# Attention rows split into a near part and a residue-class part, with their weights exchanged through DRAM

## The chip, the core and the metric

The kernel runs on one core of a Trainium2 chip. The metric is device time in microseconds (us) of one launch. The engines are named as in the profile: PE (matmul), PEld (its weight loads), DVE (vector), ACT (activation), POOL, and SP, whose queue issues nearly all DMAs.

## What is computed

One transformer-like block for 1024 tokens of width 1024: an input projection, a gated depthwise convolution branch, an attention branch with 16 heads of 64, a gated merge, an output projection, and a convolutional feed-forward part. The change touches the attention alone. The reference runs three dilated windows for each head and mixes them by their log sums:

```python
DILATION_GROUPS = ((128, 1), (512, 4), (2048, 16))
...
for window, dilation in DILATION_GROUPS:
    o_g, lse_g = dilated_window_attention(q, k, v, slopes, window, dilation)
    outs.append(o_g)
    lses.append(lse_g)
mix = jax.nn.softmax(jnp.stack(lses), axis=0)
o = jnp.einsum('gbsh,gbshd->bshd', mix, jnp.stack(outs))
```

Mixing windows by their log sums is the same as one softmax over all earlier keys, in which a key counts once for each window that holds it. So a query at token i sees key j = i - d when d <= 128, or d is a multiple of 4 and d <= 512, or d is a multiple of 16. Both kernels put the count and the distance bias into one table, the mask, which holds -1e30 where no window holds the key.

## The kernel before

All matmul operands are kept as a high and a low part (`split`: ACT copies with rounding, DVE subtracts), so that a product takes two or three matmuls. Weights come through `stage` (DMA into one of four `raw` buffers) and `wsplit`. Programs are written in loops and a scheduler then orders each engine's instructions by its own timing model, so the order on an engine is that of the built program, not of the source.

The attention stage works head by head. `head(h)` loads q, kh, kl (six DMAs), the mask m (128x1024) and v. `score(h, tiles, i)` makes the scores of query block i (128 tokens) against all its (i+1)*128 earlier keys: matmuls of up to 512 columns, with q as stationary operand and kh, then kl, as moving one. One DVE instruction adds the mask and takes the extreme of the row, ACT takes exp and the row's sum, DVE the reciprocal, and POOL scales the row. `flip` turns a tile of 128 keys: PE transposes it for up to four query blocks into one PSUM bank, and `split` writes ph and pl. `weigh` multiplies v by ph and pl into o. `step` writes the order: the four scores of a half head (512 queries) are interleaved with the flips and weighings of the half head before, with `PEND` flips between a flip and its weighing.

Between these parts stands side work, `side_work`: the gate projections that are left and the conv-output projections, one step being three matmuls of 512 columns. `fill(n)` adds n to a credit and issues one step for each whole unit. The shares of side work are `FILL = (5.5, 9.5)` for the two halves, 15 steps per head; what is left over runs after the last head:

```python
        step(None, prev)
        for _ in filler:
            pass
```

After that the next stage loads o back (`load_split(oT, do_, half, "o")`, half 0 and then half 1, four `raw` buffers each), loads and splits `w_ao`, and multiplies (`yb`).

Of the kernel before, what the change touches and what calls it, by code (L numbers as in the profile page):

```python
# [12 lines left out]
F32 = mybir.dt.float32  # L13
F32R = mybir.dt.float32r
AF = mybir.ActivationFunctionType
ALU = mybir.AluOpType
# [4 lines left out]
P = 128  # L21
# [10 lines left out]

LAG = 2
PEND = 2
FILL = (5.5, 9.5)
COVER = (24, 16, 52)


# [12 lines left out]
def block_kernel(ctx: ExitStack, tc: tile.TileContext, x, g1, g2, pack, mask,  # L51
# [22 lines left out]
    def split(hi, lo, src):  # L74

        act.activation(hi, src, AF.Copy)  # L76
        dve.tensor_tensor(out=lo, in0=src, in1=hi.bitcast(F32), op=ALU.subtract)  # L77
# [54 lines left out]
    def fetch(dst, src):  # L132
        sp.dma_start(dst.bitcast(F32), src.bitcast(F32))


    dq = [[dr.tile([P, 4, T], F32R, name=f"dq{i}_{a}") for a in range(2)] for i in range(2)]
    dk = [[dr.tile([P, 4, T], F32R, name=f"dk{i}_{a}") for a in range(2)] for i in range(2)]
# [207 lines left out]
    with tc.tile_pool(name="ph2", bufs=1) as p2:  # L345
        def side_work():
            for t in gates:
                if t == "half":
                    aT = hb_tiles(hb1, "aT")
                    load_split(aT, da, 0, "a")  # L350
                yield
            load_split(aT, da, 1, "a")
            for c0 in (0, 4):
                ws = [wpiece(w_co[c], f"co{c}") for c in range(c0, c0 + 4)]
                for half in range(2):
                    for c in range(c0, c0 + 4):
                        yp = bank_ps(f"ya_{c}_{half}")
                        yield from gemm_half(yp, ws[c - c0], aT, half)
                        ya = cst.tile([P, 512], F32, tag="f2", bufs=2, name=f"ya_{c}_{half}")
                        act.activation(ya, yp, AF.Copy)  # L360
                        sp.dma_start(dya[c][:, half * 512 : half * 512 + 512], ya)

        def head(h):
            hp, r, g8 = h // 2, (h % 2) * DH, h // 8
            q = p2.tile([P, T], F32R, tag="q", bufs=2, name=f"q_{h}")
            kh = p2.tile([P, T], F32R, tag="kh", bufs=2, name=f"kh_{h}")
            kl = p2.tile([P, T], F32R, tag="kl", bufs=2, name=f"kl_{h}")
            m = p2.tile([P, T], F32, tag="m", bufs=2, name=f"m_{h}")
# [5 lines left out]
            sp.dma_start(m, mask[h])  # L374
            fetch(v, dv[h // 8][:, h % 8, :, :])
            return q, kh, kl, v, m

        def score(h, tiles, i):
            q, kh, kl, v, m = tiles
            nk = (i + 1) * P  # L380
            s = big_ps(f"s_{h}_{i}")
            for c0 in range(0, nk, 512):
                n = min(512, nk - c0)
                pe.matmul(s[:, c0 : c0 + n], q[:, i * P : (i + 1) * P], kh[:, c0 : c0 + n], start=True, stop=False)  # L384
                pe.matmul(s[:, c0 : c0 + n], q[:, i * P : (i + 1) * P], kl[:, c0 : c0 + n], start=False, stop=True)
            pt = p2.tile([P, nk], F32, tag=f"p{i}", bufs=1, name=f"p_{h}_{i}")
            st = p2.tile([P, 32], F32, tag="st", bufs=4, name=f"st_{h}_{i}")
            u0 = 896 - i * P
            dve.tensor_tensor_reduce(out=pt, in0=s[:, :nk], in1=m[:, u0 : u0 + nk], scale=-1.0, scalar=3e38,  # L389
                                     op0=ALU.add, op1=ALU.min, accum_out=st[:, 0:1])  # L390
            act.activation(pt, pt, AF.Exp, bias=st[:, 0:1], scale=-1.0, accum_out=st[:, 1:2])  # L391
            dve.reciprocal(st[:, 2:3], st[:, 1:2])  # L392
            pool.tensor_scalar(pt, pt, st[:, 2:3], 1.0, op0=ALU.mult, op1=ALU.mult)  # L393
            return pt

        def flip(h, half, pts, kt):
            q0 = max(0, kt - half * 4)
            pp = bank_ps(f"pp_{h}_{half}_{kt}")
            for qb in range(q0, 4):
                pe.transpose(pp[:, qb * P : (qb + 1) * P], pts[qb][:, kt * P : (kt + 1) * P], ident)  # L400
            ph = p2.tile([P, 512], F32R, tag="ph", bufs=4, name=f"ph_{h}_{half}_{kt}")
            pl = p2.tile([P, 512], F32R, tag="pl", bufs=4, name=f"pl_{h}_{half}_{kt}")
            c = slice(q0 * P, 512)
            split(ph[:, c], pl[:, c], pp[:, c])
            return kt, ph, pl, c

        def weigh(o, v, nkt, kt, ph, pl, c):
            pe.matmul(o[:, c], v[:, kt, :], ph[:, c], start=(kt == 0), stop=False)  # L408
            pe.matmul(o[:, c], v[:, kt, :], pl[:, c], start=False, stop=(kt == nkt - 1))  # L409
# [11 lines left out]
        opairs = {}  # L421

        def step(cur, prev):

            pts = []
            rate = FILL[0] / 14 if prev is not None and prev[1] else FILL[1] / 10
            if prev is not None:
                h, half, ppts, v = prev
                nkt = half * 4 + 4
                o = bank_ps(f"o_{h}_{half}")  # L430
                pend = []
            for n in range(4):
                if cur is not None:
                    pts.append(score(cur[0], cur[2], cur[1] * 4 + n))
                fill(rate)
                if prev is not None:
                    for kt in range(n * nkt // 4, (n + 1) * nkt // 4):
                        pend.append(flip(h, half, ppts, kt))
                        fill(rate)
                        if len(pend) > PEND:  # L440
                            weigh(o, v, nkt, *pend.pop(0))
            if prev is not None:
                while pend:
                    fill(rate)
                    weigh(o, v, nkt, *pend.pop(0))
                r = (h % 2) * DH
                if h % 2 == 0 and half == 0:
                    opairs[h // 2] = p2.tile([P, T], F32, tag="op", bufs=2, name=f"op_{h}")
                opair = opairs[h // 2]
                tmp = p2.tile([P, 512], F32, tag="ot", bufs=2, name=f"ot_{h}_{half}")  # L450
                act.activation(tmp[r : r + DH, :], o[DH:P, :], AF.Copy)
                dve.tensor_tensor(out=opair[r : r + DH, half * 512 : half * 512 + 512], in0=o[0:DH, :],
                                  in1=tmp[r : r + DH, :], op=ALU.add)
                if h % 2 == 1:
                    sp.dma_start(do_[:, h // 2, half * 512 : half * 512 + 512],
                                 opair[:, half * 512 : half * 512 + 512])
            return pts

        prev = None
        nxt = head(0)  # L460
        for h in range(H):
            cur = nxt
            for half in range(2):
                if half == 1 and h + 1 < H:
                    nxt = head(h + 1)
                pts = step((h, half, cur), prev)
                prev = (h, half, pts, cur[3])
        step(None, prev)
        for _ in filler:
            pass  # L470

# [337 lines left out]

def _mask():  # L810

    dist = np.arange(P)[:, None] + 896 - np.arange(T)[None, :]
    cnt = ((dist <= 128).astype(np.int64) + ((dist % 4 == 0) & (dist <= 512)) + (dist % 16 == 0)) * (dist >= 0)
    base = np.where(cnt > 0, np.log(np.maximum(cnt, 1)), 0.0)
    slopes = 2.0 ** (-8.0 * np.arange(1, H + 1) / H)
    m = base[None] - slopes[:, None, None] * dist[None]
    return np.where(cnt[None] > 0, m, -1e30).astype(np.float32)


def _layout(a):  # L820
# [38 lines left out]
```

## Time and profile before

| what | value |
|---|---|
| median of 3 runs | 1814.08 us (1813.51 to 1816.09) |
| the profiled execution | 1811.43 us, span 1809.6 us |
| mean granted TensorE clock | 0.991 |
| PE busy | 1765.8 us, 98% of the span |
| DVE, ACT, POOL busy | 1318.8, 771.6 and 195.8 us |
| DMA | 257.57 MB, mean 142 GB/s |
| attention stage, first score to first `yb` matmul | 549.6 to 976.9 us |

A page row names line, engine, operation, tiles written and read, shapes and count, then the busy time of the group, the mean of one in ns, and the idle time of the engine just before them with what ended it. Matmuls are pipelined and their records overlap, so durations of PE are not to be summed.

### The profile page before, as it was taken

To read this page: it belongs to the slowest core of one execution; us is meant where nothing else is said; L and a number is where in the kernel's file an instruction comes from. 1 tells how busy PE (TensorE), PEld (TensorE's weight loads), DVE (VectorE), ACT (ScalarE), POOL (GpSimd) and SP (SyncE) were. 2 spreads that over 40 slices of the span, in tenths; PEclk is the share of its full clock that TensorE was granted. 3 is DMA by queue.
4 is the path that set the end of the run, shared out by engine and by line. 5 is a ranking of instruction groups with operands and counts; after the bars stand their busy time and mean duration, and the time that the engine had idled before them with its cause. 6 is when DMAs were issued, how large, how long until landed. Compare 5 with 4: busy or idle time off the path is not lost.

```text
span 1809.6 us, 22474 instructions
## 1 busy us (share of the span) xinstructions
PE 1765.8 (98%) x8244; PEld 1461.9 (81%) x8244; DVE 1318.8 (73%) x1798; ACT 771.6 (43%) x1202; POOL 195.8 (11%) x197
## 2 busy tenths in 40 slices
PE   7999999999999999999999999989999999999999
PEld 5888888888887888887888878768888888878887
DVE  5999999999735655666654543787777777789863
ACT  4111132232245656666655332545444554543441
POOL 1000133133002122222210000210000000000000
PEclk9999999999999999999999999999999999999999
DMA  5111145345549456666527543313222222389851
GB/s 203 59 47 47 41 134 163 116 134 157 157 173 246 145 158 175 180 165 179 164 70 279 169 160 133 104 48 107 80 82 81 71 95 91 116 303 335 298 180 47
DMA packets 142063, 257.57 MB, mean 142 GB/s; under 512 B 11265, under 2 KB 60545, under 8 KB 141953
## 3 DMA queue, kind: packets, MB, share of 16 engines
q1 hardware_dynamic: 141808, 255.61, 43.8%
q8 instruction: 65, 1.06, 0.3%
q10 hardware_dynamic: 144, 0.52, 0.1%
q14 instruction: 46, 0.37, 0.1%
HBM read 190.03 MB, written 66.06 MB: 142 GB/s over the span
## 4 chain that ended last, share of the span: by engine, by line
PE 53%; DMA 4%; DVE 4%; issue 1%; ACT 1%; SPq 1%; POOLq 0%; POOL 0%; DVEq 0%; ACTq 0%
PE xz L550 5%; PE xz L551 5%; PE xz L552 5%; PE dx L703 5%; PE dy L703 5%; DMA gg<-dya 2%; PE pp L400 2%; PE y L550 2%; PE y L552 2%; PE y L551 2%; PE ya L108 2%; PE ya L109 2%; PE ya L110 2%; PE o L408 2%; PE wo L126 1%; PE wo L127 1%
## 5 line engine op out<-in xcount | busy, mean ns | idle before, releaser
L253 DVE SCALAR_TENSOR_TENSOR cacc<-apad,pk,cacc 128x1024 f32<-128x1024 f32 x240 | 297.7, 1274 | 0.7
L125 PE MATMUL qkv<-hi_qkv,hT 128*128 128x512 f32 x384 | 151.8, 396 | 0.0
L127 PE MATMUL qkv<-hi_qkv,hT 128*128 128x512 f32 x384 | 150.0, 391 | 0.0
L126 PE MATMUL qkv<-lo_qkv,hT 128*128 128x512 f32 x384 | 149.4, 390 | 0.0
L389 DVE CUSTOM_DVE_ANT_0 p<-s,m 128x128 f32<-128x128 f32 (+7 forms) x128 | 95.1, 750 | 62.7 <-PE pp L400 39.0
L77 DVE TENSOR_TENSOR pl<-pp,ph 128x512 fp32r<-128x512 f32 x192 | 103.1, 549 | 49.1 <-ACT ph L76 48.6
L393 POOL TENSOR_SCALAR p<-p,st 128x128 f32<-128x128 f32 (+7 forms) x128 | 94.9, 748 | 335.5 <-DVE st L392 211.9
L76 ACT ACTIVATE ph<-pp 128x512 fp32r<-128x512 f32 x192 | 91.3, 487 | 92.2 <-PE pp L400 89.3
L649 DVE SCALAR_TENSOR_TENSOR u<-u,pk 128x1023 f32<-128x1023 f32 (+1 forms) x88 | 112.3, 1279 | 18.9 <-ACT u L647 18.5
L101 POOL TENSOR_TENSOR rs<-ss,mhalf 128x8 f32<-128x8 f32 (+1 forms) x40 | 80.3, 2010 | 353.1 <-DVE ss L100 353.0
L391 ACT ACTIVATE p<-p,st 128x128 f32<-128x128 f32 (+7 forms) x128 | 99.0, 776 | 14.6 <-DVE st L389 12.9
L108 PE MATMUL gate<-hT,hi_gt 128*128 128x512 f32 x256 | 101.8, 398 | 0.0
L109 PE MATMUL gate<-hT,hi_gt 128*128 128x512 f32 x256 | 100.8, 394 | 0.0
L110 PE MATMUL gate<-hT,lo_gt 128*128 128x512 f32 x256 | 100.3, 393 | 0.0
L400 PE MATMUL pp<-ident,p 128*128 128x128 f32 x576 | 94.4, 277 | 0.0
L127 PEld LDWEIGHTS qkv<-hi_qkv,hT 128*128 128x128 f32 x384 | 72.0, 188 | 15.3
L126 PEld LDWEIGHTS qkv<-lo_qkv,hT 128*128 128x128 f32 x384 | 72.2, 188 | 14.5 <-DVE lo_qkv L77 0.3
L125 PEld LDWEIGHTS qkv<-hi_qkv,hT 128*128 128x128 f32 x384 | 72.2, 188 | 14.0
L400 PEld LDWEIGHTS pp<-ident,p 128*128 128x128 f32 x576 | 69.5, 142 | 10.0 <-issue 0.2
L384 PE MATMUL s<-kh,q 128*128 128x512 f32 (+1 forms) x192 | 69.7, 368 | 7.3 <-DVE st L389 4.8
L408 PE MATMUL o<-ph,v 128*128 128x512 f32 x192 | 73.1, 381 | 3.6 <-ACT ph L76 1.8
L409 PE MATMUL o<-pl,v 128*128 128x512 f32 x192 | 70.5, 369 | 1.6 <-DVE pl L77 1.5
(269 smaller groups left out, 4610.4 us busy)
## 6 DMA issues: line engine op xcount, KB each, us to landing
wr<-w_down SPq DMA_DIRECT2D x45, 512.0 KB, 5.7
gr<-dff SPq DMA_DIRECT2D x62, 256.0 KB, 5.2
raw_qkv<-w_qkv SPq DMA_DIRECT2D x24, 512.0 KB, 3.9
raw_uv<-w_up SPq DMA_DIRECT2D x22, 512.0 KB, 3.3
raw_ug<-w_up SPq DMA_DIRECT2D x22, 512.0 KB, 3.3
dff<-u SPq DMA_DIRECT2D x22, 512.0 KB, 2.6
dv<-v SPq DMA_DIRECT2D x16, 512.0 KB, 3.2
raw_gt<-w_ch SPq DMA_DIRECT2D x16, 512.0 KB, 4.8
```

The lines of the kernel that those rows point to most:

```text
L108: pe.matmul(o, hi[:, k, :], ah[:, k, :], start=(k == 0), stop=False)
L109: pe.matmul(o, hi[:, k, :], al[:, k, :], start=False, stop=False)
L110: pe.matmul(o, lo[:, k, :], ah[:, k, :], start=False, stop=(k == KT - 1))
L125: pe.matmul(ps, ah, hi[:, k % 2, :], start=(k == 0), stop=False)
L126: pe.matmul(ps, ah, lo[:, k % 2, :], start=False, stop=False)
L127: pe.matmul(ps, al, hi[:, k % 2, :], start=False, stop=(k == KT - 1))
L253: dve.scalar_tensor_tensor(out=acc, in0=a[:, j : j + T], scalar=w(j), in1=acc, op0=ALU.mult, op1=ALU.add)
L400: pe.transpose(pp[:, qb * P : (qb + 1) * P], pts[qb][:, kt * P : (kt + 1) * P], ident)
L550: pe.matmul(o, wh[:, k, :], bh[:, k, :], start=(start and k == 0), stop=False, skip_group_check=not start)
L551: pe.matmul(o, wh[:, k, :], bl[:, k, :], start=False, stop=False, skip_group_check=not start)
L552: pe.matmul(o, wl[:, k, :], bh[:, k, :], start=False, stop=(k == 3), skip_group_check=not start)
L703: pe.matmul(banks[n], a[:, c], b[:, d], start=(start and i == 0 and m == 0), stop=(stop and i == nf - 1 and m == 2), skip_group_check=True)
```

## The change

Keys are parted in two. The near part of query block i holds the keys of its own block and of the block before (at most 256), with the distances up to 128. The far part holds the keys at a distance over 128, all of which are a multiple of 4 away, so that a query needs only keys of its own residue modulo 4. For each residue r the 256 queries and 256 keys of that class are read straight out of q, kh and kl with a step of 4 elements, as two blocks of 128 queries against 96 and 224 keys (`FAR` = 224).

- Each part has its own softmax, with its own extreme and sum. The two must be joined: far statistics are laid out by residue class, near ones by token, and the order is changed by way of DRAM. Per head, one DMA stores the far statistics and four load them by token; DVE and ACT work out a weight for each part and row; one DMA stores the far weights and four load them by class; POOL then scales the sixteen parts.
- The mask shrinks to 480 columns, and the far values `vf` are loaded again by class, with eight more DMAs per head.
- Flips of near tiles write their result in class order (`by_class`, `by_token`), so that near and far weighings add into one bank; the exit of o turns the order back, and each half head has its own store.
- A head's order is now: far scores, near scores, exchange, scaling; then the flips and weighings of the head before. The shares of side work are `FILL = (9.0, 9.0)`, 18 steps per head.

The diff, cut to its core:

```diff
-FILL = (5.5, 9.5)
+FILL = (9.0, 9.0)
+NEAR, FAR = 256, 224
...
+    dst = [[dr.tile([P, 16], F32, name=f"dst{i}_{a}") for a in range(2)] for i in range(H)]
...
+            vf = p2.tile([P, 4, 2, P], F32R, tag="vf", bufs=2, name=f"vf_{h}")
...
+            for a in range(4):
+                for b in range(2):
+                    fetch(vf[32 * a : 32 * a + 32, :, b, :],
+                          dv[h // 8][:, h % 8, 4 * b + a, :].rearrange("(j r) d -> j r d", r=4))
...
+        def near(h, tiles, u, st, pts):
+            s = big_ps(f"sn_{h}_{u}")
+            for n in range(4):
...
+                bank.matmul(s[:, c], q[:, i * P : (i + 1) * P], kh[:, k], False)
+                bank.matmul(s[:, c], q[:, i * P : (i + 1) * P], kl[:, k], True)
+                softmax_part(s[:, c], pt[:, c], m[:, NEAR - nk : NEAR], st[:, n, u, :])
...
+        def far(h, tiles, u, st, pts):
+            cls = lambda t, r, k0, k1: t.rearrange("p (k r) -> p r k", r=4)[:, r, k0:k1]
+            for b in (1, 0):
+                for c in range(2):
...
+                    for kx, last in ((kh, False), (kl, True)):
+                        bank.matmul(sv, cls(q, r, b * P, b * P + P), cls(kx, r, 0, nk), last)
+                    softmax_part(sv, pc, m[:, NEAR + FAR - nk : NEAR + FAR], st[:, r, b, :])
...
+        def scores(h, tiles):
+            for u in range(2):
+                yield from far(h, tiles, u, sf, pts)
+            sp.dma_start(dst[h][0], sf.rearrange("p r b x -> p (r b x)"))
+            for a in range(4):
+                sp.dma_start(sts[:, 1, a, :, :],
+                             dst[h][0][32 * a : 32 * a + 32, :].rearrange("j (r b x) -> j r b x", r=4, b=2))
+            for u in range(2):
+                yield from near(h, tiles, u, sts[:, 0], pts)
...
+            sp.dma_start(dst[h][1][:, 0:8], e[:, 1])
+            for a in range(4):
+                sp.dma_start(wf[32 * a : 32 * a + 32, :, :],
+                             dst[h][1][:, 2 * a : 2 * a + 2].rearrange("(j r) b -> j r b", r=4))
...
+        for h in range(H + 1):
+            if h < H:
+                cur = nxt
+                for pts in scores(h, cur):
+                    fill(FILL[0] / 16)
+                if h + 1 < H:
+                    nxt = head(h + 1)
+            if prev is not None:
+                for _ in weighing(h - 1, *prev):
+                    fill(FILL[1] / 14)
+            prev = (pts, cur[3], cur[4])
```

More of the change, by code (lines that the diff above doesn't have):

```diff
@@ L367, in head @@
             kl = p2.tile([P, T], F32R, tag="kl", bufs=2, name=f"kl_{h}")
-            m = p2.tile([P, T], F32, tag="m", bufs=2, name=f"m_{h}")
+            m = p2.tile([P, 512], F32, tag="m", bufs=2, name=f"m_{h}")
             v = p2.tile([P, 8, P], F32R, tag="v", bufs=2, name=f"v_{h}")
+            vf = p2.tile([P, 4, 2, P], F32R, tag="vf", bufs=2, name=f"vf_{h}")
             for s in range(2):
@@ L373, in head @@
                 fetch(kl[s * DH : (s + 1) * DH, :], dk[g8][1][r : r + DH, hp % 4, :])
-            sp.dma_start(m, mask[h])
+            sp.dma_start(m[:, : NEAR + FAR], mask[h])
             fetch(v, dv[h // 8][:, h % 8, :, :])
[L376 to L389, printed above, removed]
+            for a in range(4):
+                for b in range(2):
+                    fetch(vf[32 * a : 32 * a + 32, :, b, :],
+                          dv[h // 8][:, h % 8, 4 * b + a, :].rearrange("(j r) d -> j r d", r=4))
@@ L390, in score, with softmax_part @@
+        def softmax_part(s, pt, m, st):
+            dve.tensor_tensor_reduce(out=pt, in0=s, in1=m, scale=-1.0, scalar=3e38,
                                      op0=ALU.add, op1=ALU.min, accum_out=st[:, 0:1])
             act.activation(pt, pt, AF.Exp, bias=st[:, 0:1], scale=-1.0, accum_out=st[:, 1:2])
[L392 to L405, printed above, removed]
@@ L419, in fill, with weighing @@
                 next(filler, None)
[L421 to L429, printed above, removed]
+        def weighing(h, pts, v, vf):
+            for half in range(2):
                 o = bank_ps(f"o_{h}_{half}")
+                bank = Bank()
                 pend = []
[L432 to L442, printed above, removed]
+                todo = list(pieces(pts, v, vf, o, half))
+                for n, (name, parts, moves) in enumerate(todo):
+                    pend.append((flip(h, name, parts), moves, n == len(todo) - 1))
+                    yield
+                    if len(pend) > PEND:
+                        weigh(bank, *pend.pop(0))
+                        yield
@@ L443, in step @@
                 while pend:
-                    fill(rate)
-                    weigh(o, v, nkt, *pend.pop(0))
+                    weigh(bank, *pend.pop(0))
+                    yield
                 r = (h % 2) * DH
[L447 to L457, printed above, removed]
+                sum_ = p2.tile([P, 512], F32, tag="ot", bufs=2, name=f"ot_{h}_{half}")[r : r + DH, :]
+                act.activation(by_token(sum_), by_class(o[DH:P, :]), AF.Copy)
@@ L459, in block_kernel @@
+                dve.tensor_tensor(out=by_token(sum_), in0=by_class(o[0:DH, :]), in1=by_token(sum_), op=ALU.add)
+                sp.dma_start(do_[r : r + DH, h // 2, half * 512 : half * 512 + 512], sum_)
         prev = None
         nxt = head(0)
[L461 to L464, printed above, removed]
+        for h in range(H + 1):
[4 more added lines that the diff above has]
+                if h + 1 < H:
```

119 lines of the change are left out of this document (108 added, 11 removed).

## The prediction

> **What bounds the kernel now.** I read the page first (busy shares, then the chain that ended last), then the windows of the attention stage, then the timeline of PE inside it and across its end.
>
> ```profile
> span 1809.6 us, 22474 instructions
> PE 1765.8 (98%) x8244; PEld 1461.9 (81%) x8244; DVE 1318.8 (73%) x1798; ACT 771.6 (43%) x1202; POOL 195.8 (11%) x197
> PE 53%; DMA 4%; DVE 4%; issue 1%; ACT 1%; SPq 1%; POOLq 0%; POOL 0%; DVEq 0%; ACTq 0%
> ```
>
> PE is busy for 98% of the span and leads the chain, so a microsecond of PE saved counts and a microsecond in which PE stands idle is paid in full. The change touches only the stage from the first score matmul (549.6 us) to the first matmul of the attention output projection (976.9 us). The windows view gives, for that stretch, its length and then the busy times of PE, PEld, DVE, ACT, POOL, the granted clock and the DMA share:
>
> ```profile
> 549.60:976.90 427.30, 416.62 (x2208) 350.21 (x2209) 260.65 (x645) 266.30 (x557) 94.91 (x128) 0.98 0.60 175
> ```
>
> Nothing but PE is near full here. Matmul records overlap (a 0.39 us record every 0.23 us), so what a matmul costs is the distance between starts. The timeline of PE (start, length, line) shows it for each width:
>
> ```profile
> 841.95 0.22 PE L384 MATMUL s<-kh,q 128*128 128x128 f32 x1
> 842.01 0.28 PE L385 MATMUL s<-kl,q 128*128 128x128 f32 x1
> 842.12 0.28 PE L408 MATMUL o<-ph,v 128*128 128x128 f32 x1
> 842.23 0.28 PE L409 MATMUL o<-pl,v 128*128 128x128 f32 x1
> 842.34 1.06 PE L400 MATMUL pp<-ident,p 128*128 128x128 f32 x8
> 843.16 0.48 PE L384 MATMUL s<-kh,q 128*128 128x512 f32 x1
> ...
> 843.71 0.28 PE L384 MATMUL s<-kh,q 128*128 128x256 f32 x1
> 843.83 0.28 PE L385 MATMUL s<-kl,q 128*128 128x256 f32 x1
> 843.95 0.39 PE L408 MATMUL o<-ph,v 128*128 128x512 f32 x1
> ...
> 849.22 0.39 PE L108 MATMUL ya<-aT,hi_co 128*128 128x512 f32 x1
> ...
> 853.07 0.39 PE L110 MATMUL ya<-aT,lo_co 128*128 128x512 f32 x1
> ```
>
> 512 columns: 17 steps from 849.22 to 853.07, 0.226 us each. 256 columns: 0.12. 128 columns: 0.06 for the first after a wide one (841.95 to 842.01), then 0.11 in a row (842.01, .12, .23, .34). Transposes: eight in 0.82, 0.103 each. 384 columns lie between 512 and 256, some 0.17 (an estimate). The 0.11 is a floor: halving 256 columns saves hardly anything, since each matmul brings its own 128-column weight load.
>
> **PE work removed and added, for one head.** Before: scores are 24 matmuls (12 of 512, 4 each of 384, 256 and 128 columns): 12x0.226 + 4x0.17 + 4x0.12 + 2x0.06 + 2x0.11 = 4.21 us. The weighing has the same widths, 4.21. Transposes 36x0.103 = 3.71. Sum 12.13, and 194.1 over 16 heads. After: near scores are 14 matmuls of 256 and 2 of 128 columns, 1.90; far scores 8 of 224 and 8 of 96 columns, all at the floor if their step of 4 is free, 16x0.11 = 1.76; transposes 27x0.103 = 2.78; near weighing 10 of 256 and 10 of 128, 2.30; far weighing 24 of 128 columns, 2.64. Sum 11.38, and 182.1 over 16 heads. The columns fall by 28% (18,432 to 13,312), the PE time by 6%: **-12.0 us**.
>
> [...]
>
> **Side work and what is lost now.** The built order of PE has 864 side matmuls (gate and conv-output projections) between the first score and the output projection before, and 861 after: 195 us of 0.226 each, unchanged. So attention now takes 427.3 - 195.3 = 232.0 where its rows add up to 194.1. The other 37.9 us are weight loads exposed after a wait and short idles (427.3 - 416.6 = 10.7 is plain idle). I leave these 37.9 as they are: flips get smaller, but there are more of them.
>
> **The end of the stage.** In the order before, the last weighing matmul is followed by 125 side matmuls; in the order after by none: the new shares (18 side steps per head instead of 15) use them up inside the heads. What those 125 hide is in the rows of PE and ACT there:
>
> ```profile
> 948.39 0.28 PE L409 MATMUL o<-pl,v 128*128 128x128 f32 x1
> 948.70 0.59 ACT L451 ACTIVATE ot<-o 64x512 f32<-64x512 f32 x1 [4.83 <-PE o L409]
> 952.18 3.91 ACT L76 ACTIVATE oT<-raw_o 128x1024 fp32r<-128x1024 f32 x4 [1.68 <-DMA do<-op]
> ...
> 961.76 1.06 ACT L76 ACTIVATE oT<-raw_o 128x1024 fp32r<-128x1024 f32 x1 [0.64 <-DMA raw_o<-do]
> ...
> 971.07 1.06 ACT L76 ACTIVATE hi_ao<-raw_ao 128x1024 fp32r<-128x1024 f32 x1 [1.42 <-DMA raw_ao<-w_ao]
> ...
> 976.91 0.39 PE L108 MATMUL yb<-oT,hi_ao 128*128 128x512 f32 x1
> ```
>
> From the last weighing matmul, the store of o, its reload in two halves, the splits and only then (the raw buffers are shared) the weights w_ao take until 971.07 + 1.06 = 972.13: 23.7 us after 948.39. PE worked on side matmuls all that time. After the change the same instructions stand in the same order with nothing over them: **+23.7 us** of idle PE. Bounds: some 20 if the half-0 reloads are early, 26 if the transfers crowd.
>
> The last head pays the exchange too, since the far weights travel through DRAM and no next head's scores remain. Rows for the small steps, first of ACT, then DVE, POOL and DMA (the last column of a DMA row is issue to landing):
>
> ```profile
> L391 ACT ACTIVATE p<-p,st 128x256 f32<-128x256 f32 x16 | 8.1, 506 | 0.1
> L391 ACT ACTIVATION_READ_ACCUMULATOR p<-p,st 128x1 f32 x128 | 24.4, 190 | 0.0
> L76 ACT ACTIVATE ph<-pp 128x512 fp32r<-128x512 f32 x96 | 56.2, 595 | 50.5 <-PE pp L400 48.4 <-PE o L409 0.6
> L389 DVE CUSTOM_DVE_ANT_0 p<-s,m 128x256 f32<-128x256 f32 x16 | 6.7, 418 | 6.8 <-PE s L385 6.6
> L389 DVE DVE_READ_ACCUMULATOR2_ANT st<- 128x1 f32 x128 | 10.5, 82 | 0.0
> L392 DVE RECIPROCAL st<-st 128x1 f32<-128x1 f32 x128 | 19.9, 157 | 16.1 <-ACT p L391 15.3
> L77 DVE TENSOR_TENSOR pl<-pp,ph 128x512 fp32r<-128x512 f32 x96 | 64.9, 686 | 28.9 <-ACT ph L76 28.5
> L393 POOL TENSOR_SCALAR p<-p,st 128x256 f32<-128x256 f32 x16 | 7.7, 478 | 21.1 <-DVE st L392 15.7 <-PE o L409 5.2
> do<-op SPq DMA_DIRECT2D x16, 256.0 KB, 2.3
> m<-mask SPq DMA_DIRECT2D x16, 512.0 KB, 8.4
> 704.73 0.59 SPq L133 DMA_DIRECT2D kh<-dk  x1
> ...
> 709.10 0.33 SPq L133 DMA_DIRECT2D v<-dv  x1
> ```
>
> After the last near score: 0.42 + 0.08 on DVE, 0.51 + 0.19 on ACT, six small DVE steps at 0.16 and a small exp of some 0.3, together 2.5; a store (0.33 + 2.3), four loads (4x0.37 + 2.3), 8.9 in all; eight far scalings on POOL, below 0.48 each (some 0.4, an estimate), 12.1; the last two flips (transposes 0.4, then 0.60 + 0.69, the second split 0.69 later) and their matmuls, some 15. PE has 27 transposes, 44 weighing and 6 side matmuls for that time, 2.8 + 4.9 + 1.4 = 9.1. So **+6 us** more idle; bounds 0 and, with landings of 8.4 instead of 2.3, 18. Inside the stage the same exchange is hidden: head h is weighed only after the scores of head h+1 and the weighing of h-1, a whole head's period.
>
> **The step of 4.** No row of before has a PE operand with a step, so I bound it. From below nothing. From above: a stepped read may cost as much as reading the whole span; 128 stepped columns span 512 and the weight load, which paces the narrow matmuls at 0.11, would take 0.44; 224 moving columns span 896, at 0.226/512 per column 0.40, which hides behind that. So 256 far matmuls cost between 0 and 256 x 0.33 = 84.5 us more. I take half rate, the middle in ratio between free and four times: the weight load at 0.22 (the 224 moving columns at 0.20 hide behind it), so 0.22 for each far matmul instead of 0.11, **+28.2 us**.
>
> **Covered.** ACT, per head: 16 exps with reads, at most 16x(0.506+0.19) = 11.1, seven evictions at most 4.2, the two exits of o 1.2, and of side work a split and two exits, some 2.5: 19.0. DVE: 16x0.50, six small, seven splits, two adds, 8.0 + 0.9 + 4.8 + 1.4, and 2 of side work: 17.1. POOL: at most 16x0.478 = 7.6. The period of PE will be (195 + 182 + 28 + 38)/16 = 27.7. If the stepped reads of the near flips and of o cost double, ACT is at 22.6 and DVE at 21.2, still covered. The DVE step that takes the far statistics waits for a DMA; behind it on DVE stand the splits of the head before, for whom PE would wait; its cover is the eight near parts. SP issues 28 DMAs per head for 9 or so before (8 for vf, 10 for the exchange); that is the third rival.
>
> **The sum.** The profiled execution took 1811.4 us (span 1809.6): -12.0 + 23.7 + 6 + 28.2 = +45.9, so 1857.3 beside it. The median of the runs, 1814.1, lies 2.7 above that execution, so I predict **1860**.
>
> **Rivals.** (1) Stepped operands are free on PE: +17.7, 1832. For it: the weight load is slow per column as it is (0.11 for 128), which may leave room. (2) Faster: stepped operands are free and the 37.9 us of exposed waits go, because the flip of a key tile no longer holds PE up (ACT waited 48.4 us for pp, and PE takes the results at once). All of it gone gives 17.7 - 37.9 = -20.2, 1794; it decides from 17.7 of the 37.9. Against it: more and narrower dependent steps. (3) SP sets the pace. Its issues take 6x0.64 + 25x0.37 = 13.1 per head (28 and three of side work), and it stands still for two stores of the exchange until they land, as the loads behind them read what they wrote. At 2.3 each it is at 17.7 and hidden; at 8.4, behind a head's loads in the same queue, 29.9, which is 2.2 per head over PE: +35, 1895. It decides from 7.3 us a landing. [...]
>
> **How the numbers follow.** Forecast 0.34; (1) 0.31; (2) 0.13; (3) 0.15; (4) 0.07. The range leaves out (2) and (4), 0.20 together: from 1815 ((1) without the last head's 6 and with 11 of the 37.9 gone) to 1902 ((3), with 7 for a crowded end). A measurement of this kernel tells about 0.2% from no change. Faster by more than that is (2), 0.13; the lower edge of (1) gives within 0.2% a chance of 0.04; slower 0.83.
>
> **What would show it.** [...] An idle PE of 20 to 30 us right before the first yb matmul, released by hi_ao, confirms the end; without it I am wrong by as much. SP with no idle time in mid-stage, and PE waits on q, kh or vf loads, would show (3). A stage shorter than 427 us would make the whole prediction wrong.

## The result and the profile after

| kernel | median of the runs | ratio to the kernel before (95% interval) | profiled span | granted clock |
|---|---|---|---|---|
| before | 1814.4 us (1813.5 to 1816.1) | 1 | 1809.6 us | 0.991 |
| after | 1932.1 us (1930.4 to 1937.4) | 1.0652 (1.0630 to 1.0675) | 1928.5 us | 0.961 |

One execution of the kernel with neither step nor exchange (below) took 8488 us where its three others took 1838 to 1842; it is left out of that kernel's median, and as it was the profiled one, no trace of that kernel is read.

The change costs 118 us, 6.5%. I had forecast 1860 us, at most 1902: the direction was right, the size was not. On the page of the kernel after, PE stands idle more (94% of the span against 98%) and DMA has 12% of the chain that ended last, against 4%:

```profile
span 1928.5 us, 23872 instructions
PE 1813.3 (94%) x8548; PEld 1519.3 (79%) x8548; DVE 1305.9 (68%) x1942; ACT 788.0 (41%) x1394; POOL 211.7 (11%) x325
PE 75%; DMA 12%; DVE 5%; ACT 2%; issue 2%; SPq 2%; POOL 1%; POOLq 0%; DVEq 0%; ACTq 0%
```

In the windows view of the kernel after (start and end, length, then the busy times of PE, PEld, DVE, ACT, POOL, the granted clock, of which 1.00 is full speed, DMA share), the first row is the whole attention stage, from the first far score to the first `yb`; the second ends with the last weighing matmul:

```profile
551.80:1092.30 540.50, 458.65 (x2510) 404.33 (x2510) 243.39 (x786) 281.22 (x747) 112.35 (x256) 0.88 0.55 144
551.80:1069.30 517.50, 458.56 (x2509) 404.28 (x2509) 230.85 (x773) 266.20 (x730) 112.35 (x256) 0.90 0.53 137
```

The stage takes 540.5 us instead of 427.3, 113.2 more; of those 23.0 lie behind the last weighing matmul, where PE does nothing. The other 90 are in the heads, where I had expected 22 (-12.0 + 6 + 28.2). The waits of PE in the kernel after (waiting instruction, what it waited for, us in total, times, longest) name two large ones:

```profile
PE pp_f L497 <- POOL pf L482: 29.2, 10, 5.1
PE yb L109 <- DMA raw_ao<-w_ao: 22.9, 1, 22.9
...
PE sf L400 <- DVE sf L410: 8.3, 4, 7.0
```

The second is the end of the stage, forecast at 23.7. The first is not in my prediction: in ten places the flips of far weights wait for POOL, which scales them. One of them in the timeline of the kernel after (start, length, engine, line, idle before and its releaser in brackets; the PE and POOL rows of the far part and the small DMAs):

```profile
932.41 0.18 DVE L476 TENSOR_TENSOR ew<-ew,mx 128x16 f32<-128x16 f32 x1
...
934.23 0.52 SPq L478 DMA_DIRECT2D dst<-ew  x1
...
937.41 0.41 PE L400 MATMUL sf<-kl,q 128*128 128x96 f32 x1
...
938.29 2.50 SPq L480 DMA_DIRECT2D wf<-dst  x4
...
942.53 3.01 POOL L482 TENSOR_SCALAR pf<-pf,wf 128x96 f32<-128x96 f32 x8 [6.20 <-DMA wf<-dst]
...
942.93 0.45 PE L497 MATMUL pp_f<-ident,pf 128*96 128x128 f32 x1 [5.11 <-POOL pf L482]
```

The merged weights are ready at 932.59. Their store is issued 1.6 us later and the loads that read it wait until it has landed, at 938.29; they land, and POOL begins at 942.53, 9.9 us after the merge. By 937.82 PE has finished what stands ahead of the far flips in its order: side work, near flips and 12 of the next head's 16 far score matmuls, and none of its 16 near ones. Then it stands still for 5.1 us. It is so in most heads: in 11 of the 15 heads that have a next one, none of the next head's near score matmuls stands ahead of the far flips. In one head all 32 score matmuls do, and there PE does not wait. The landings of the exchange in the stage (KB each, median us from issue to landing) are slower for the stores than the 2.3 us that I took:

```profile
wf<-dst SPq DMA_DIRECT2D x64, 1.0 KB, 2.1
...
dst<-ew SPq DMA_DIRECT2D x16, 4.0 KB, 4.4
```

### The profile page after: what moved, and what is told of

Same layout as the page of the kernel before. It is cut to its first block, busy times and chain, and to the rows that moved or that the text cites. A ratio compares the mean times of both kernels' runs of the same rounds, so it can differ in the third digit from the quotient of the medians.

```text
span 1928.5 us, 23872 instructions
## 1 busy us (share of the span) xinstructions
PE 1813.3 (94%) x8548; PEld 1519.3 (79%) x8548; DVE 1305.9 (68%) x1942; ACT 788.0 (41%) x1394; POOL 211.7 (11%) x325
## 4 chain that ended last, share of the span: by engine, by line
PE 75%; DMA 12%; DVE 5%; ACT 2%; issue 2%; SPq 2%; POOL 1%; POOLq 0%; DVEq 0%; ACTq 0%
PE xz L660 5%; PE xz L661 5%; PE xz L662 5%; PE qkv L126 5%; PE qkv L128 5%; PE qkv L127 5%; PE dy L813 4%; PE o L400 4%; PE dx L813 4%; DMA dst<-ew 2%; PE gate L109 2%; PE gate L110 2%; PE gate L111 2%; PE y L660 2%; PE y L661 2%
## 5 line engine op out<-in xcount | busy, mean ns | idle before, releaser
L410 DVE CUSTOM_DVE_ANT_0 pf<-sf,m 128x224 f32<-128x224 f32 (+1 forms) x128 | 40.2, 321 | 106.9 <-PE sf L400 93.5
L410 DVE CUSTOM_DVE_ANT_0 pn<-sn,m 128x256 f32<-128x256 f32 (+1 forms) x128 | 49.5, 404 | 80.4 <-PE sn L400 79.6
L482 POOL TENSOR_SCALAR pn<-pn,ew 128x256 f32<-128x256 f32 (+1 forms) x128 | 63.6, 518 | 365.1 <-DVE ew L476 279.4
L412 ACT ACTIVATE pn<-pn,sts 128x256 f32<-128x256 f32 (+1 forms) x128 | 62.4, 489 | 73.7 <-DVE sts L410 73.3
L109 PE MATMUL yb<-oT,hi_ao 128*128 128x512 f32 x128 | 51.1, 399 | 22.9 <-DMA raw_ao<-w_ao 22.9
L412 ACT ACTIVATE pf<-pf,sf 128x224 f32<-128x224 f32 (+1 forms) x128 | 54.0, 423 | 39.4 <-DVE sf L410 38.4
L660 PE MATMUL xz<-h2left,hi_uv 128*128 128x512 f32 x176 | 68.7, 390 | 0.8 <-ACT hi_uv L77 0.8
L662 PE MATMUL xz<-h2left,lo_uv 128*128 128x512 f32 x176 | 68.6, 390 | 0.0
L660 PE MATMUL xz<-blk_t,hi_s3g 128*128 128x512 f32 x176 | 68.5, 389 | 0.0
L661 PE MATMUL xz<-h2left,hi_uv 128*128 128x512 f32 x176 | 68.5, 389 | 0.0
```

What stands on the lines that cost most here:

```text
L109: pe.matmul(o, hi[:, k, :], ah[:, k, :], start=(k == 0), stop=False)
L660: pe.matmul(o, wh[:, k, :], bh[:, k, :], start=(start and k == 0), stop=False, skip_group_check=not start)
L661: pe.matmul(o, wh[:, k, :], bl[:, k, :], start=False, stop=False, skip_group_check=not start)
L662: pe.matmul(o, wl[:, k, :], bh[:, k, :], start=False, stop=(k == 3), skip_group_check=not start)
```

## The experiments

Each kernel is the changed kernel with one to three edits, unless it says otherwise. Times are medians. The kernel before ran again beside each set of experiments, with medians of 1812.1 to 1814.2 us, so a difference of some 2 us between kernels of different sets says nothing. The scheduler orders an edited kernel anew (without the exchange, for instance, the far flips of the sixth head stand behind 16 far score matmuls instead of 8), so an edit's price holds together with the order that was made for it.

### 1. No step of 4

```diff
-cls = lambda t, r, k0, k1: t.rearrange("p (k r) -> p r k", r=4)[:, r, k0:k1]
+cls = lambda t, r, k0, k1: t[:, r * 256 + k0 : r * 256 + k1]
```

> The far scores read q, kh and kl as contiguous columns (same number and widths of matmuls; the choice of the class of the token is left out, so the far weights are those of other tokens). My account now: the 256 far matmuls start 0.235 us apart instead of 0.11 to 0.12, some 32 us in all, and the stage loses that much: 1932 - 32 = 1900 us, from 1890 to 1910 as the clock and the waits shift with it. If the step costs nothing and the 0.235 is only a wait for something else: 1932, no change. If the waits for the exchange take up what PE gains, since PE then arrives earlier at the same far flips: 1915 to 1930. In the trace the far starts should be 0.11 to 0.12 us apart.

Measured: 1927.9 us (1925.9 to 1932.1), 4 less, which the spread of the runs hardly tells from nothing. The starts did fall (the median from a kl score of 224 columns to the next start is 0.114 us instead of 0.236), and PE's busy time with them, but its idle time grew by as much or more. The windows view of this kernel up to the last weighing matmul, and its waits:

```profile
551.30:1071.60 520.30, 443.16 (x2509) 385.37 (x2509) 229.14 (x773) 263.06 (x730) 114.25 (x256) 0.87 0.53 137
```

```profile
PE pp_f L497 <- POOL pf L482: 40.0, 11, 6.0
...
PE sf L400 <- DVE sf L410: 12.7, 8, 8.9
```

Busy 443.2 instead of 458.6, idle 77.1 instead of 58.9, clock 0.87 instead of 0.90. My account was wrong and the third expectation right: the next head's far scores are part of what covers the exchange, so that a cheaper far score is a shorter cover. The step cannot be priced while the exchange is there.

### 2. No exchange; shares cut for the end; far flips behind the next scores

No exchange (both DMA round trips taken out):

```diff
-                yield from far(h, tiles, u, sf, pts)
+                yield from far(h, tiles, u, sts[:, 1], pts)
-            sp.dma_start(dst[h][0], sf.rearrange("p r b x -> p (r b x)"))
-            for a in range(4):
-                sp.dma_start(sts[:, 1, a, :, :],
...
+            wf = e[:, 1].rearrange("p (a b) -> p a b", b=2)
-            sp.dma_start(dst[h][1][:, 0:8], e[:, 1])
-            for a in range(4):
-                sp.dma_start(wf[32 * a : 32 * a + 32, :, :],
```

> The exchange through DRAM is left out (10 DMAs per head less; the far statistics go straight into the merge, and the far weights are used in the order in which they were made, so that they belong to other tokens). All matmuls, flips, scalings and small DVE steps stay. Theory A (the exchange's latency lies on PE's path in every head, because the far flips of a head stand soon after its own near scores in PE's order): the 52 us of idle PE in mid-stage and 6 of the last head's 8 go, and with the idle gaps the stretches at half clock, 15 to 30 us: 1932 - 75 to - 88, 1844 to 1857 us. Theory B (the flips wait for the POOL scalings themselves, or for the merge on DVE, and the exchange only happens to stand ahead of these): the gaps stay, 1915 to 1930. Theory C (the clock sinks because matmuls are narrow, not because PE idles): the gaps go and the clock stays at 0.90 in the stage, 1932 - 58 = 1874.

Measured: 1863.4 us, 68.7 less: theory A's mechanism, but outside its range (1844 to 1857), as less was won than it said. No wait on POOL's far scalings is left in the windows of 453.4 us up to the last weighing:

```profile
552.00:1005.40 453.40, 440.94 (x2509) 394.00 (x2509) 230.66 (x773) 266.00 (x730) 110.50 (x256) 0.94 0.59 155
```

Against the kernel after, the same 2509 matmuls have 12.5 us of idle time instead of 58.9 (46.5 less) and are 17.6 us shorter busy, at a clock of 0.94 instead of 0.90; together the 64.1 us by which this stretch is shorter.

Shares cut:

```diff
-FILL = (9.0, 9.0)
+FILL = (7.5, 7.5)
```

> The shares of the side work are cut from 9.0 + 9.0 to 7.5 + 7.5 steps a head, so that 132 side matmuls are left behind the last head's weighing, as in the kernel before (125). Theory: these cover the 23 us between the last weighing matmul and the first matmul of the output projection, and PE comes to that projection without the half clock of the idle stretch: 1932 - 23 to - 30, 1902 to 1909 us. Rival: the side work is missing inside the heads, where it covered part of the exchange, and the waits there grow by as much as the end saves: 1925 to 1935.

Measured: 1912.8 us, 19.3 less, between the theory (1902 to 1909) and the rival. The 23 us at the end are covered; mid-stage waits for far flips rose a little (33.5 us against 29.2).

Far flips behind the next scores: an ordering edge on PE from the last near score of head h+1 to the far flips of head h.

```diff
+                t = pe.transpose(pp[:nk, i * P : (i + 1) * P], part, ident)
+                if name[0] == "f" and h + 1 in last_score:
+                    tc.add_manual_dep(t.ins, last_score[h + 1].ins.name,
+                                      mybir.DependencyInfo(mybir.DependencyClass.NoSync, mybir.DependencyReason.DATA),
+                                      reason="far flips behind the next scores")
```

> One kind of ordering edge is added and nothing else: on PE the far flips of head h stand behind the last near score of head h+1, which is where my prediction took them to be. Theory A: the exchange is then hidden by a head's scores; the mid-stage gaps (52 us) and the half clock that follows them (15 to 30 us) go, the last head's exchange, the end and the step stay: 1932 - 67 to - 82, 1850 to 1865 us. Rival B: the wait moves on: the buffers of the weighted parts are held longer, DVE or POOL then hold PE up elsewhere, and less than a third is won: 1910 to 1932.

Measured: 1901.0 us, 31 less: between the two expectations. The far flips no longer wait but for one, in the first head; instead the next head's scores, now in one stretch, wait for DVE to empty their banks (waits of PE in this kernel):

```profile
PE sn L400 <- DVE sts L413: 12.5, 26, 2.1
...
PE pp_f L500 <- POOL pf L485: 3.3, 1, 3.3
```

So the place in the order is a cause, and moving it does not win back all of the exchange.

### 3. Step and exchange together, and what is left

Neither step nor exchange (both edits above):

> Both edits together: no step of 4 in the far scores and no exchange through DRAM (the choice of the class and the reordering of the weights are left out). With the exchange in place the step's removal gave 4 us only, though the far starts went from 0.235 to 0.11 and 0.16; PE waited 11 us more for the far flips and 4 more for the far scores' banks. Theory: without the exchange PE is the bound again and the step is paid in full, 256 x (0.235 - 0.12) = 29 us: 1863 - 29 = 1834, from 1828 to 1840. Rival (the step is covered whatever stands beside it, the banks of the far scores being what PE waits for): 1855 to 1863.

Measured: 1839.9 us (the median of three runs), 23.6 less than without the exchange alone. With the exchange away the step costs, as the theory said, though less than its 29. What covers the rest is not shown; in the trace of the next kernel but one, which has neither step nor exchange, the far scores wait 6.4 us for their banks, against 1.7 in the kernel without the exchange, which would fit.

Exchange issued and not used: the ten DMAs go to buffers that nobody reads.

```diff
...
-                sp.dma_start(sts[:, 1, a, :, :],
+                sp.dma_start(sf[:, a, :, :],
...
-                sp.dma_start(wf[32 * a : 32 * a + 32, :, :],
+                sp.dma_start(wd[32 * a : 32 * a + 32, :, :],
```

> All ten DMAs of the exchange are issued as in the changed kernel, on the same queue and with the same waits of that queue, but what they bring is not used: the merge and the scalings read the values where they were made (so the reordering of the weights is left out). Theory A (PE waits for the exchange's latency): near the kernel without the exchange, 1863 to 1870 us. Theory B (my third rival: the ten issues and the stores that the queue stands still for hold up the loads of q, kh, kl, vf and the stores of o): 1900 to 1932.

Measured: 1877.0 us, 55.1 less than the changed kernel and 13.6 more than without the DMAs; outside both expectations and near A. So 55 of the 68.7 us are waiting for the values, 14 what the DMAs cost that nobody waits for. Of the 14, one wait shows: the first conv-output weights, behind these DMAs in SP's queue, came late. It takes 10.4 us in this kernel, 1.8 without the DMAs, but only 3.5 in the kernel after, so part of the 14 belongs to this kernel alone (waits of PE in this kernel):

```profile
PE ya L109 <- ACT hi_co L77: 10.4, 1, 10.4
```

Neither step nor exchange, and shares of 7.5 + 7.5:

> No step, no exchange, and shares of 7.5 + 7.5, so that side matmuls cover the end (class and reordering left out): all three costs away, the narrow near and far parts stay. My first sum has -12 us for what is left: 1800. Theory (three causes, additive once the exchange is away): 1834 - 19 to - 23, 1811 to 1815, which is the time of the kernel before; the -12 is then lost to the matmuls' other spacings. Rival (a fourth cause, the clock under narrow matmuls, which runs at 0.94 in the stage without the exchange against 0.98 before): 1820 to 1835.

Measured: 1821.5 us, 18.3 less than with the full shares. That is the rival's lower end: 7.4 us over the kernel before (ratio 1.0041, 1.0027 to 1.0056) where my sum had -12. The windows up to the last weighing matmul, first of this kernel, then of the kernel before:

```profile
551.60:959.40 407.80, 388.47 (x2386) 340.71 (x2386) 228.39 (x773) 257.20 (x724) 111.25 (x256) 0.95 0.64 171
```

```profile
549.60:948.40 398.80, 388.12 (x2083) 326.59 (x2083) 244.89 (x630) 247.10 (x532) 94.91 (x128) 0.98 0.58 164
```

Idle time is 19.3 us against 10.7, 8.6 more; busy time is equal where some 12 less were due, at a clock of 0.95 against 0.98. So the narrow parts bring 9 us of extra waits (mostly of the scores for their banks, 10.2 us against 4.8). The clock accounts for the 12 by an estimate from these rows: 0.03 of 388 us is 11.7.

The kernel before without its cover at the end:

```diff
-FILL = (5.5, 9.5)
+FILL = (6.6, 11.4)
```

> The kernel before, its shares of side work set from 5.5 and 9.5 to 6.6 and 11.4, so that no side matmul is left behind the last head's weighing; nothing else. It prices the end alone, without the new attention: the idle PE should be the 23 to 24 us of the rows, 1812 + 21 to + 27: 1833 to 1839 us. Rival (the side work inside the heads fills exposed waits there and gives part of it back): 1815 to 1828.

Measured: 1839.0 us, 24.9 more, at the upper end of the forecast, and one wait of PE that was not there:

```profile
PE yb L108 <- DVE oT L77: 21.7, 1, 21.7
```

The end is priced without any of the new attention: 125 side matmuls did cover it.

### 4. Which exchange, which operand, and both remedies

Statistics not exchanged (first half of the edit of the no-exchange kernel):

> Only the first of the two exchanges is left out (the far maxima and sums to the near rows; the merge takes them in the order in which they were made); the weights still go out and back. Theory A: this one is covered, since it is issued before the eight near parts and only the merge on DVE waits for it: 1915 to 1930 us. Rival B: each of the two costs half of the 69 us: 1890 to 1905.

Measured: 1920.0 us, 12.1 less: theory A.

Weights not exchanged (second half of it):

> Only the second of the two exchanges is left out (the far weights back to the far rows; the scalings take them in the order in which they were made); the statistics still go out and back. Theory A: this is the one that PE waits for, with nothing between the merge and the far flips to cover it: most of the 69 us goes, 1865 to 1885 us. Rival B: each costs half, 1890 to 1905.

Measured: 1887.9 us (1883 to 1897), 44.2 less, just over theory A's upper end. The weights' way out and back is the one that PE waits for; the statistics' way is mostly covered by the near parts, but not wholly. In the kernel after, DVE waits three times, 14.0 us in all, for the loads of the statistics, and the far scores' wait of 8.3 us for DVE to empty their banks (7.0 of it in one place) is 1.3 us in the kernel without this exchange and 12.9 us in the one that keeps it alone. The two gains make 56, less than the 68.7 of both; this may be because either wait hides part of the other, which no run shows.

Stationary operand contiguous, no exchange:

```diff
+flat = lambda t, r, k0, k1: t[:, r * 256 + k0 : r * 256 + k1]
...
-bank.matmul(sv, cls(q, r, b * P, b * P + P), cls(kx, r, 0, nk), last)
+bank.matmul(sv, flat(q, r, b * P, b * P + P), cls(kx, r, 0, nk), last)
```

> The kernel without the exchange, and of the far scores' operands only the stationary one (q) contiguous; the moving keys keep their step of 4 (class and reordering left out). My forecast's step: the weight load sets the 0.22 us and the moving columns hide behind it. Theory A (so it is): the far starts fall to 0.11 to 0.16 us and the time to that of the kernel with neither step nor exchange, 1841, from 1836 to 1848. Rival B (the moving operand pays too): starts of 224 columns stay at 0.2 and above, those of 96 columns fall, 1848 to 1858. Rival C (the moving operand alone pays): 1863.

Measured: 1846.4 us, against 1863.4 with both operands stepped and 1839.9 with none: in its time theory A, but in its starts rival B. The timelines of PE, of the kernel after and of this one, price each operand:

```profile
935.60 0.42 PE L400 MATMUL sf<-kl,q 128*128 128x224 f32 x1
935.83 0.42 PE L400 MATMUL sf<-kh,q 128*128 128x224 f32 x1
936.07 0.42 PE L400 MATMUL sf<-kl,q 128*128 128x224 f32 x1
...
936.94 0.42 PE L400 MATMUL sf<-kl,q 128*128 128x96 f32 x1
937.17 0.42 PE L400 MATMUL sf<-kh,q 128*128 128x96 f32 x1
937.41 0.41 PE L400 MATMUL sf<-kl,q 128*128 128x96 f32 x1
```

```profile
709.42 0.37 PE L400 MATMUL sf<-kh,q 128*128 128x224 f32 x1
709.61 0.38 PE L400 MATMUL sf<-kl,q 128*128 128x224 f32 x1
709.81 0.38 PE L400 MATMUL sf<-kh,q 128*128 128x224 f32 x1
...
711.73 0.33 PE L400 MATMUL sf<-kh,q 128*128 128x96 f32 x1
711.88 0.29 PE L400 MATMUL sf<-kl,q 128*128 128x96 f32 x1
```

With q stepped the starts are 0.23 to 0.24 apart whatever the width, so the stepped weight load sets them; with q contiguous 224 stepped moving columns take 0.19 to 0.21, and 96 columns 0.15 after a bank's change, 0.112 as the median of those on kl. So the moving operand pays as well (0.204 as the median of 224 columns on kl, against 0.114 without a step), and this shows only once the weight load no longer sets the pace.

Both remedies that keep the whole computation (the ordering edge and shares of 7.5 + 7.5):

> The whole computation, with the two remedies that keep it whole: the far flips of a head behind the next head's near scores on PE, and shares of 7.5 + 7.5 of the side work. Alone they gave 31 and 19 us. If they add up: 1932 - 50 = 1882, from 1876 to 1888 us. If both draw on the same cover (side work taken out of the heads was hiding what is left of the exchange): 1888 to 1900.

Measured: 1879.5 us: they add up. It is still 3.6% over the kernel before (ratio 1.0362, 1.0339 to 1.0386). Since the kernel with all three costs taken out (1821.5) is no faster than the kernel before, no version of this split was in sight that would be.

### 5. Does idle time halve the clock?

One gap in the timeline of PE in the kernel after, and the windows of that kernel before it, behind it, and after that:

```profile
740.82 0.40 PE L111 MATMUL gate<-hT,lo_gt 128*128 128x512 f32 x1
743.36 1.09 PE L497 MATMUL pp_f<-ident,pf 128*96 128x128 f32 x3 [2.14 <-POOL pf L482]
...
745.67 0.41 PE L400 MATMUL o<-ph_n,v 128*128 128x256 f32 x1
745.88 0.41 PE L400 MATMUL o<-pl_n,v 128*128 128x256 f32 x1
```

```profile
735.00:741.20 6.20, 6.20 (x31) 4.99 (x29) 1.24 (x7) 1.82 (x6) 2.89 (x7) 1.00 0.46 84
743.40:750.10 6.70, 6.70 (x33) 6.37 (x33) 2.20 (x11) 2.79 (x9) 2.57 (x7) 0.51 0.85 186
750.10:757.00 6.90, 6.90 (x46) 6.11 (x44) 3.54 (x10) 3.68 (x11) 0.00 (x0) 1.00 0.35 86
```

PE stands still for 2.14 us; the 6.7 us that follow run at 0.51 of the clock, 256 columns start 0.21 apart instead of 0.12, and then the clock is whole again. The end shows it more cleanly, since the same `yb` matmuls come there with and without an idle stretch ahead of them. These are the windows of the first 3.7 us from the first `yb` on, in the kernel after (22.9 us idle before), in the kernel before (not idle), and in the kernel before without its cover (21.7 us idle):

```profile
1092.30:1096.00 3.70, 3.66 (x8) 2.45 (x9) 3.59 (x3) 2.13 (x3) 0.00 (x0) 0.50 0.80 269
976.90:980.60 3.70, 3.70 (x18) 3.06 (x17) 1.25 (x2) 1.53 (x2) 0.00 (x0) 1.00 0.88 290
1004.70:1008.40 3.70, 3.66 (x8) 2.46 (x9) 3.61 (x3) 2.59 (x3) 0.00 (x0) 0.50 0.86 262
```

So half clock followed the idle stretches of 22.9, 21.7 and 2.14 us alike.

A gap is not the only occasion. In the kernel after the clock is also half from 831.9 to 849.0, and in the ten us before that PE was idle for 0.3 us only; they end in a row of eight far scores with stepped operands. The windows before and behind:

```profile
822.00:831.90 9.90, 9.59 (x51) 8.33 (x49) 4.46 (x20) 5.13 (x11) 2.24 (x6) 1.00 0.66 156
831.90:841.00 9.10, 6.28 (x22) 4.99 (x22) 7.88 (x25) 7.07 (x25) 5.84 (x11) 0.50 0.32 80
```

To see how much the gaps cause in mid-stage, matmuls without use, on the head's v (`warm`), were put ahead of the first far flip of each head; the flips then overwrite the bank. The edit with 8 (the other has 16):

```diff
+            if name == "f00":
+                for _ in range(8):
+                    pe.matmul(pp, warm[:, 0, :], warm[:, 0:4, :].rearrange("p a b -> p (a b)"), start=True, stop=True)
```

> The whole computation of the changed kernel, and for each head 8 matmuls of 512 columns without use on PE, shortly ahead of the first far flip (into the bank that the flip then overwrites): 128 x 0.227 = 29 us of PE. By the gaps ahead of the first far flips (4.6, 4.0, 1.2, 1.5, 2.1, 3.0, 5.1, 2.3, 0.9, 4.8 us) 16 of the 29 us lie in idle time and 13 are added. Theory A (idle gaps cause the half clock): the half clock in the stage falls from 100 us (127 less 27 at the end) to 60 or lower, and gives back 15 to 20: 1925 to 1932, no slower in spite of the added work. Theory B (it comes with the narrow matmuls or by chance): the clock stays at 0.90 and the time is 1932 + 13 = 1945, from 1940 to 1950.

> As before with 16 matmuls without use per head, 58 us of PE; by the same gaps 26 of them lie in idle time and 32 are added. Theory A: hardly a gap is left in mid-stage, the half clock there falls below 50 us and gives back 25 to 35: 1930 to 1940. Theory B: 1932 + 32 = 1964, from 1958 to 1970.

Measured: 1937.4 and 1950.2 us, 5 and 18 more: between the theories both times. The windows up to the last weighing, of 8 and of 16:

```profile
550.80:1075.40 524.60, 483.83 (x2637) 423.50 (x2637) 234.00 (x773) 267.40 (x730) 113.44 (x256) 0.92 0.52 136
```

```profile
551.20:1090.50 539.30, 508.12 (x2764) 442.66 (x2765) 232.74 (x773) 269.91 (x730) 109.09 (x256) 0.93 0.51 132
```

The clock rises from 0.90 to 0.92 and 0.93. Busy time grows by 25.3 and 49.6 us where the added matmuls take 29 and 58 at 0.227 each, so by this estimate the others became 3.8 and 8.5 us faster. Filling gaps does give clock back, though less than theory A said. How much of the rest comes from the gaps that were left (40.8 and 31.2 us idle) and how much from narrow matmuls as such stays open.

## Why the prediction was wrong

By the experiments the 118 us are: exchange 68.7 (55.1 waiting for the values, 13.6 the rest), step 23.6, end 18.3, the narrow parts 7.4. They were taken away one after the other, and the sum is 118.0; in another order the shares shift, as the first experiment shows.

**The step that failed** is the sentence "Inside the stage the same exchange is hidden: head h is weighed only after the scores of head h+1 and the weighing of h-1, a whole head's period." That is the order in which the program is written. In the built order, which the scheduler makes, the far flips of head h stand behind some of the far scores of head h+1, and PE gets there in 5 us, while the weights take 9.9. I had counted PE's matmuls in the built order, but had not looked where the far flips stand in it. My sum had 6 us for the exchange, in the last head alone; the runs give 68.7. That the kernel without the exchange, 1863.4, lies 3.4 from my 1860 is luck. Without those 6 us my sum is 1854 for it, and the 9.4 between are errors that partly cancel: the narrow parts 19.4 too low, the end 5.4 and the step 4.6 too high.

**The landing** of an exchange store was taken as 2.3 us, of a 256 KB store; it took 4.4. The third rival (SP sets the pace from 7.3 us a landing) did not come about: with all DMAs issued and nobody waiting the time is 1877. SP does stand still for the stores (46.9 and 44.8 us in the kernel whose exchange is issued and not used), and that and the ten issues are worth some 14 us in that kernel.

**Idle PE was priced at its own length.** The 46.5 us of waiting in mid-stage came with 17.6 us of slower matmuls. No term for the clock was in the sum: it took the stage's 0.98 as it was for a stage with gaps, where it fell to 0.90.

**-12.0** did not come: with all other costs away it is +7.4. "I leave these 37.9 as they are" is the sentence behind it; the scores wait for their banks 10.2 us instead of 4.8, and the clock falls to 0.95. The floor of 0.11 itself held: without a step the medians behind the kl scores are 0.112 and 0.114.

**The end, +23.7**: right. The wait is 22.9 us, and it is worth 19.3 in the changed kernel, 18.3 with step and exchange away, 24.9 in the kernel before.

**The last head, +6**: right in size; the waits of PE in it add up to 7.2 us (1.69, 4.80 and 0.74).

**The step of 4, +28.2**: the mechanism was right, the weight load sets the pace at 0.235 us (0.22 forecast) and 224 moving columns at 0.204 (0.20) hide behind it. Rival (1), with 0.11, is out, and so is the upper bound of 0.44. It is worth 23.6 once PE is the bound, and 4 or nothing while the exchange is. The cost is a factor of about 2 for a step of four fp32 elements (0.236 us between starts against 0.114), not the whole span.

**Covered work** stayed covered: DVE is busy for 231 and ACT for 266 of 517 us, though the exits of o took up to 1.8 times as long (below). One part of that paragraph failed: the eight near parts do not cover the statistics in every head, and DVE's 14.0 us of waiting for them held the far scores up (8.3 us, 1.3 with that exchange left out). Rival (2), faster, is out: the exposed waits grew.

## What to carry to other kernels

A latency is hidden by what stands between its start and its use in the built order of the waiting engine, not in the program (here 5 us of cover for 9.9 us); count those matmuls before calling it covered. If the cover is itself something that you mean to make cheaper, the gain turns into waiting (the step was worth 4 us with the exchange and 23.6 without), and only with the wait taken away do the other prices show. An idle gap of PE can cost more than its length, but no fixed rate came out. Taking the exchange away saved 17.6 us of busy PE with 46.5 us of idle, 0.4 for each. Filling gaps saved some 0.2 and 0.3 (3.8 with 18.2, 8.5 with 27.8). The ordering edge saved nothing: 28.6 us less idle, at 458.8 us of busy PE against 458.6.

## What the runs showed of the hardware

A step of 4 cost nothing in one place and made instructions 1.6 to 1.8 times as long in another. In the stage of the kernel after, ACT and DVE read stepped PSUM at the full rate (the near flips' rows, 594 and 684 ns; 595 and 686 before without a step). With the stepped side in SBUF, which ACT writes and DVE reads and writes, the exits of o took 1093 and 1084 ns; before, without a step and with the same shape, 594 and 682. No run steps a write to PSUM on these engines, so memory and direction are not told apart:

```profile
L562 ACT ACTIVATE ot<-o 64x512 f32<-64x512 f32 x31 | 33.9, 1093 | 18.3 <-PE o L400 17.8
L563 DVE TENSOR_TENSOR ot<-o,ot 64x512 f32<-64x512 f32 x31 | 33.6, 1084 | 36.5 <-ACT ot L562 35.6 <-DMA dya<-ya 0.8
L78 DVE TENSOR_TENSOR pl_n<-pp_n,ph_n 128x512 fp32r<-128x512 f32 x48 | 32.3, 684 | 9.7 <-ACT ph_n L77 9.5
...
L77 ACT ACTIVATE ph_n<-pp_n 128x512 fp32r<-128x512 f32 x48 | 28.0, 594 | 22.5 <-PE pp_n L497 22.0
```

And a store of 4 KB landed later (4.4 us) than the store of o, of 256 KB in the kernel before (2.3 us) and of 128 KB in the kernel after (2.4 us): the time to landing of these small stores isn't set by their bytes. With the other exchange left out the small stores took 3.2 (of 8 KB) and 3.6 us (of 4 KB); what sets the time stays open.
